# A block pair's first sum and block A22's low part by negated copies and adding DMAs, two more block pairs, and modulation kept off the late tiles

## The chip, the cores and the metric

The kernel runs on one core of a Trainium2 chip. Its engines work side by side, each in the order of its own queue: TensorE (PE) multiplies, VectorE (DVE) and ScalarE (ACT) do elementwise work, GpSimd (POOL) does a little in the attention, SyncE (SP) issues most of the loads, and 16 DMA engines carry them out. The metric is the device time of one execution in microseconds; lower is better.

## What is computed

The reference is a two-layer block stack (width 1024, 256 latent tokens and 256 context tokens). Layer 0 has a short-convolution mixer, layer 1 a grouped-query attention; before and after each mixer stands a gated feed-forward network (FFN). Every step is modulated by vectors that come from `c` and `c_ctx` through `mod_w`. Cut to what matters:

```python
mod  = (silu(c)     @ mod_w[i] + mod_b[i])       # 9 vectors of 1024 per layer, per stream
modc = (silu(c_ctx) @ mod_w[i] + mod_b[i])
h    = rms(t, norm_g) * (1 + scale) + shift      # scale, shift: two of the nine
y    = (silu(h @ w13[:, :2816]) * (h @ w13[:, 2816:])) @ w2
t    = t + 0.5 * gate * y                        # FFN; gate: a third one
t    = t + gate * mixer(h)                       # conv mixer (layer 0), attention (layer 1)
```

Four FFNs run for the latents, three of them for the context as well. The nine vectors of a layer are called channels 0 to 8 here: (shift, scale, gate) for FFN, mixer, FFN. Channels 2 and 8 are the gates with the factor 0.5.

## The kernel before, in words

All of it is float32 in accuracy: a matrix is split in a high part rounded to the format that TensorE takes (`hi`, a ScalarE copy) and a low part (`lo = src - hi`, a VectorE subtraction); a product is three matmuls, `hi*hi`, `hi*lo`, `lo*hi` (`mm3`, lines 127 to 133). `split` (lines 107 to 109) makes the two parts. Tokens are the moving side, 512 of them (256 latents beside 256 context tokens) in all FFNs but the last.

**Weights.** `load_raw` takes one of 8 buffers with the tag `wr` (128 x 1024 float32, 512 KB) and lets SP load it. The parts go to `wh` and `wl`, 4 buffers each, and for block A22 to `w4h`, `w4l`, 2 each.

**FFN.** `ffn` cuts the 22 hidden blocks of 128 in thirds of 8, 7 and 7 (`THIRDS`). For each block the gate and up halves of w13 are multiplied with h, `silu(gate)*up` becomes one entry of `gs`, and `project` multiplies the entries of a third with w2 in 8 output tiles m = 0 to 7 and adds them to x in `finish` (line 547). In the last third the two last tiles are done in halves, first the 256 latents, then the context (`late`), so that the next norm (`tail_norm`) can begin.

**Block pairs.** A hidden block is done in one of two ways. As it is: 8 k-slices x 2 halves x 3 matmuls of 512 columns, 48 in all (`w13_mm`). As a pair (class `Pair`): the gate and up halves and the two halves of k make a 2 x 2 block matrix A, the streams and the halves of k a matrix B, and seven block products instead of eight are done (`head`, `five`, `six`, `seven`, `four`), 84 matmuls of 256 columns. A pair needs sums of blocks: `S1` (line 702), `S2` (703), `S3` and `S4` (711), each then split; `T1` to `T4` of the B side are made once for an FFN. Its two raw tiles are r1 = (A21, A11) and r2 = (A22, A12). `AS_IS` says which blocks of the first third are done as they are: 3 to 7 in the first FFN (blocks 0 to 2 belong to the start), none elsewhere, where blocks 0 and 1 are done as they are by hand. That makes 54 pairs.

**Modulation.** A unit is one dot product of 1024 for 128 outputs of one channel and stream on VectorE (`mod_unit`, line 173, tile `junk`); 218 of them run through the queue `jobs`, 4 (later 2) to a job, and each job loads 1 MB into two `wr` buffers. `tick(n)` adds n to what is owed and issues that many units at that place of the program; `mod_ready` issues what is missing of a channel. `tick(ev)` stands behind every tile of `project` but the late ones, `tick(4)` behind a block done as it is, `tick(5)` behind a tile of the convolution, `tick(0.5)` behind a pair.

The order of the instructions on an engine is fixed when the program is built: a planner takes, by its own times, what is ready, the earlier in the program the sooner. The start (up to 60 us) and the attention heads have an order written by hand. At run time an engine that waits for one instruction holds all behind it.

Of the kernel before, what the change touches and what calls it, by code (L numbers as in the profile page):

```python
# [9 lines left out]
F32 = mybir.dt.float32  # L10
# [13 lines left out]

AS_IS = {(0, 0): range(3, 8), (0, 1): (), (1, 0): ()}

# [21 lines left out]
def hybrid_kernel(ctx: ExitStack, tc: tile.TileContext, a: dict, out: bass.AP):  # L48
# [58 lines left out]
    def split(hi, lo, src):  # L107
        nc.scalar.activation(out=hi, in_=src, func=AF.Copy)  # L108
        return nc.vector.tensor_tensor(out=lo, in0=src, in1=hi.bitcast(F32), op=ALU.subtract)  # L109

    def half():

        return tuple(
            wp.tile([P, 1024], F32R, name=nm(t), tag=t, bufs=4) for t in ("wh", "wl")
        )
# [51 lines left out]
    def mod_unit(l, ch, pair, raw, j, v):  # L167

        mt = mod_tile(l, ch)
        kt = pair * 2 + j  # L170
        col = ch * KT + kt
        junk = mp.tile([P, D], BF16, name=nm("junk"), tag="junk", bufs=1)
        nc.vector.tensor_tensor_reduce(  # L173
            out=junk,
            in0=raw[j],
            in1=scbc[:, v, :],
            scale=1.0,
            scalar=modb[:, l, col : col + 1],
            op0=ALU.mult,
            op1=ALU.add,  # L180
            accum_out=mt[:, kt, v : v + 1],
        )
        done[l, ch] += 1
# [49 lines left out]
    def gate_of(l, j):  # L233
        m = mod_ready(l, 3 * j + 2)
        if j == 1:
            return m
        t = const.tile([P, KT, 2], F32, name=f"G{l}{j}", tag=f"G{l}{j}")
        nv = 1 if (l, j) == (1, 2) else 2
        nc.vector.tensor_scalar(
            out=t[:, :, :nv], in0=m[:, :, :nv], scalar1=0.5, scalar2=None, op0=ALU.mult  # L240
        )
        return t

# [303 lines left out]
    def finish(m, ps, c0, c1, gate, tail, wide=False):  # L547
        g = gate()
        for s in range(2):
            for o in [s * S - c0] if not wide else range(0, T2 if s == 0 else 0, S):  # L550
                if not c0 <= s * S < c1:
                    continue
                nc.vector.scalar_tensor_tensor(  # L553
                    out=x[:, m, s * S : s * S + S],
                    in0=ps[:, o : o + S],
                    scalar=g[:, m, s : s + 1],
                    in1=x[:, m, s * S : s * S + S],
                    op0=ALU.mult,
                    op1=ALU.add,
                )  # L560
        if tail:
            tail(m, c0, c1)
# [6 lines left out]
    def project(ws, src, nk, gate, tail, tot, late, ev, between=()):  # L569
# [37 lines left out]
        for m in range(nf, KT - late):  # L607
# [6 lines left out]
            finish(m, ps, 0, tot, gate, tail, wide)  # L614
            tick(ev)
        if late:
# [58 lines left out]
    class Pair:  # L675
# [6 lines left out]
        def __init__(self, src, h):  # L682
            self.h, self.w = h, {}
            self.raw = [load_raw(src[:, c : c + 1024]) for c in (0, 1024)]
            ts = half()
# [10 lines left out]
        def sums(self, n):  # L696
# [4 lines left out]
            if n == 0:  # L701
                tt(out=s1, in0=s1, in1=r2[:, :T2], op=ALU.subtract)
                tt(out=s2, in0=s2, in1=s1, op=ALU.subtract)
# [4 lines left out]
            ]  # L708
            split(*self.w["A22"], r2[:, :T2])
            v = lambda t: t.rearrange("p (a c) -> p a c", a=2)  # L710
# [42 lines left out]

    def ffn(l, b, h, tot, gate, tail, gs=(), ev=1.5, z=None):
        gs = list(gs)
        i0 = 0
        for t, n in enumerate(THIRDS):
            between = ()
            if tot == T2:
# [22 lines left out]
                for i in range(len(gs), n):  # L782
                    if t == 0 and not heads and i in AS_IS[l, b]:
# [14 lines left out]
                        w13_post(pp, gs[-1], 0, T2)  # L798
                        tick(4)
                        continue  # L800
# [46 lines left out]
            def ws2(m):  # L847
# [12 lines left out]
                else lambda k, c0, c1: (cur[k][0][:, c0:c1], cur[k][1][:, c0:c1]), n,  # L860
                gate, tail if end else None, tot, 2 if end and tot == T2 else 0, ev, between,
            )
            gs = []

    def lazy_gate(l, j):
        box = []

        def get():
            if not box:
                box.append(gate_of(l, j))  # L870
            return box[0]

        return get

# [172 lines left out]
    for i in range(3):  # L1047
        gs0.append(new_pair("g"))
        w13_post(pps[i], gs0[i], 0, T2)

    with tc.issue_after(rows["last"]):
        convk = cload("convk", [P, 3, KT])
# [6 lines left out]
    hn = Plain()  # L1059
    ffn(0, 0, h, T2, lazy_gate(0, 0), tail_norm(0, 1, hn), gs0, 2)  # L1060
    h = hn

    zs = []
    for m in range(KT):
# [4 lines left out]
        for c0, c1 in ((0, S), (S, T2)) if m == 0 else ((0, T2),):  # L1069
# [13 lines left out]
        d = tp.tile([P, T2], F32, name=nm("d"), tag="gm", bufs=3)  # L1083
        nc.vector.tensor_scalar(
            out=d, in0=u, scalar1=convk[:, 1, m : m + 1], scalar2=None, op0=ALU.mult
        )
        u2 = u.rearrange("p (s t) -> p s t", s=2)
# [15 lines left out]
    def by_pairs(key, box=None):  # L1103
# [236 lines left out]
    with tc.manual_schedule(engines={e.engine for e in (nc.tensor, nc.vector, nc.scalar, nc.gpsimd)}):  # L1340
# [31 lines left out]
    project(  # L1372
        by_pairs("wo", wos), lambda k, c0, c1: aos[k], KT, lazy_gate(1, 1), tail_early(1, 2, hn, hz), S, 0, 0,
    )
    ffn(
        1, 1, hn, S, lazy_gate(1, 2),
        lambda m, c0, c1: nc.sync.dma_start(out[m], x[:, m, :S]), z=hz,
# [81 lines left out]
```

## Time and profile before

| | |
|---|---|
| median of 3 runs | 1571.84 us (1570.1 to 1575.39) |
| the profiled execution | 1571.47 us |
| its span, first to last instruction | 1569.7 us |
| granted TensorE clock, mean | 0.998 |
| busy: TensorE / VectorE / ScalarE / GpSimd | 1557.7 / 1333.4 / 733.8 / 25.4 us |
| DMA: moved, mean rate | 248.80 MB, 159 GB/s |

Matmuls overlap in the records (a row shows 0.28 us for one that starts 0.12 us after the one before), so TensorE's busy time says only that no long hole is left in it; the start-to-start time of matmuls gives their pace, and the views by stage show where holes and a lower clock are. The queue of a stage can be full on VectorE without costing time; what counts is which wait ends last before a matmul.

### The profile page before, as it was taken

To read this page: it belongs to the slowest core of one execution; us is meant where nothing else is said; L and a number is where in the kernel's file an instruction comes from. 1 tells how busy PE (TensorE), PEld (TensorE's weight loads), DVE (VectorE), ACT (ScalarE), POOL (GpSimd) and SP (SyncE) were. 2 spreads that over 40 slices of the span, in tenths; PEclk is the share of its full clock that TensorE was granted. 3 is DMA by queue.
4 is the path that set the end of the run, shared out by engine and by line. 5 is a ranking of instruction groups with operands and counts; after the bars stand their busy time and mean duration, and the time that the engine had idled before them with its cause. 6 is when DMAs were issued, how large, how long until landed. Compare 5 with 4: busy or idle time off the path is not lost.

```text
span 1569.7 us, 25671 instructions
## 1 busy us (share of the span) xinstructions
PE 1557.7 (99%) x10210; PEld 1422.0 (91%) x10210; DVE 1333.4 (85%) x2129; ACT 733.8 (47%) x1213; POOL 25.4 (2%) x20
## 2 busy tenths in 40 slices
PE   9999999999999999999999999999999999999999
PEld 7888998999888899989899899999899889898888
DVE  5998789899997698978989989969978887887676
ACT  5622452545322365435345465435345445674553
POOL 0000000000000000000000000000000002300000
PEclk9999999999999999999999999999999999999999
DMA  9675246355565323542533614533733853366562
GB/s 373 224 237 180 89 132 187 107 173 159 194 209 166 114 75 108 177 146 87 189 126 117 196 41 135 187 108 118 239 112 114 265 154 106 123 207 221 171 199 75
DMA packets 72120, 248.80 MB, mean 159 GB/s; under 512 B 9024, under 2 KB 10816, under 8 KB 72000
## 3 DMA queue, kind: packets, MB, share of 16 engines
q1 hardware_dynamic: 69408, 245.40, 48.0%
q10 hardware_dynamic: 2592, 1.76, 0.4%
q8 instruction: 80, 1.31, 0.3%
q14 instruction: 40, 0.33, 0.1%
HBM read 244.77 MB, written 1.05 MB: 157 GB/s over the span
## 4 chain that ended last, share of the span: by engine, by line
PE 88%; DVE 6%; DMA 2%; ACT 2%; issue 1%; POOL 0%; POOLq 0%; SPq 0%; ACTq 0%; DVEq 0%
PE py L131 8%; PE py L132 8%; PE py L133 8%; PE p L131 6%; PE p L133 6%; PE p L132 6%; PE q L133 5%; PE q L131 4%; PE q L132 4%; PE py L139 2%; PE pu L139 2%; PE pg L139 2%; PE pg L132 1%; PE pg L133 1%; DMA wr<-in_w 1%; PE pu L132 1%
## 5 line engine op out<-in xcount | busy, mean ns | idle before, releaser
L108 ACT ACTIVATE wh<-wr 128x1024 fp32r<-128x1024 f32 (+2 forms) x442 | 393.7, 916 | 361.9 <-PE py L132 119.6
L109 DVE TENSOR_TENSOR wl<-wr,wh 128x1024 fp32r<-128x1024 f32 (+2 forms) x442 | 454.5, 1048 | 95.1 <-ACT wh L108 76.2
L173 DVE CUSTOM_DVE_ANT_0 junk<-wr,scbc,modb 128x1024 bf16<-128x1024 f32 x218 | 279.4, 1282 | 15.2 <-DMA wr<-in_modT 13.1
L131 PE MATMUL py<-gh,wh 128*128 128x512 f32 (+1 forms) x570 | 214.7, 377 | 0.0
L132 PE MATMUL py<-gl,wh 128*128 128x512 f32 (+1 forms) x570 | 214.0, 375 | 0.0
L133 PE MATMUL py<-gh,wl 128*128 128x512 f32 (+1 forms) x570 | 213.9, 375 | 0.0
L133 PEld LDWEIGHTS py<-gh,wl 128*128 128x128 f32 x570 | 108.3, 190 | 19.0
L131 PEld LDWEIGHTS py<-gh,wh 128*128 128x128 f32 x570 | 108.5, 190 | 18.4
L132 PEld LDWEIGHTS py<-gl,wh 128*128 128x128 f32 x570 | 108.5, 190 | 18.2
L131 PE MATMUL p<-th,wh 128*128 128x256 f32 x432 | 122.3, 283 | 0.0
L132 PE MATMUL p<-tl,wh 128*128 128x256 f32 x432 | 122.3, 283 | 0.0
L133 PE MATMUL p<-th,wl 128*128 128x256 f32 x432 | 122.2, 283 | 0.0
L553 DVE SCALAR_TENSOR_TENSOR x<-py,G,x 128x256 f32<-128x256 f32 x189 | 83.5, 479 | 36.3 <-PE py L133 25.1
L133 PE MATMUL q<-bh,wl 128*128 128x256 f32 x320 | 91.5, 286 | 0.1
L131 PE MATMUL q<-bh,wh 128*128 128x256 f32 x320 | 90.9, 284 | 0.4 <-ACT wh L108 0.4
L132 PE MATMUL q<-bl,wh 128*128 128x256 f32 x320 | 90.5, 283 | 0.0
L132 PEld LDWEIGHTS p<-tl,wh 128*128 128x128 f32 x432 | 82.8, 192 | 0.3
L131 PEld LDWEIGHTS p<-th,wh 128*128 128x128 f32 x432 | 82.8, 192 | 0.3
L133 PEld LDWEIGHTS p<-th,wl 128*128 128x128 f32 x432 | 82.8, 192 | 0.0
L108 ACT ACTIVATE w4h<-wr 128x512 fp32r<-128x512 f32 x54 | 33.8, 625 | 75.1 <-DMA wr<-in_w 56.9
L108 ACT ACTIVATE gh<-gm 128x512 fp32r<-128x512 f32 x66 | 41.6, 630 | 56.0 <-DVE gm L751 53.8
L711 DVE TENSOR_TENSOR wr<-wr,wr 128x1024 f32<-128x1024 f32 x54 | 66.0, 1222 | 0.7
(303 smaller groups left out, 3946.3 us busy)
## 6 DMA issues: line engine op xcount, KB each, us to landing
wr<-in_w SPq DMA_DIRECT2D x176, 512.0 KB, 4.5
wr<-in_modT SPq DMA_DIRECT2D x122, 512.0 KB, 4.5
wr<-in_w2b SPq DMA_DIRECT2D x64, 448.0 KB, 3.9
wr<-in_w2a SPq DMA_DIRECT2D x32, 512.0 KB, 4.7
pm<-in_mod SPq DMA_DIRECT2D x16, 512.0 KB, 10.2
wr<-in_cw_cx SPq DMA_DIRECT2D x16, 512.0 KB, 4.7
wr<-in_cw_b SPq DMA_DIRECT2D x8, 512.0 KB, 4.4
wr<-in_cw_out SPq DMA_DIRECT2D x8, 512.0 KB, 3.9
```

Of the source, the lines that this page charges most:

```text
L108: nc.scalar.activation(out=hi, in_=src, func=AF.Copy)
L109: return nc.vector.tensor_tensor(out=lo, in0=src, in1=hi.bitcast(F32), op=ALU.subtract)
L131: nc.tensor.matmul(ps, wh, mh, start=first, stop=False, **kw)
L132: nc.tensor.matmul(ps, wh, ml, start=False, stop=False, **kw)
L133: nc.tensor.matmul(ps, wl, mh, start=False, stop=last, **kw)
L139: nc.tensor.matmul(ps, w[0], m[2], start=first and n == 0, stop=False)
L173: nc.vector.tensor_tensor_reduce(out=junk, in0=raw[j], in1=scbc[:, v, :], scale=1.0, scalar=modb[:, l, col : col + 1], op0=ALU.mult, op1=A ...
L553: nc.vector.scalar_tensor_tensor(out=x[:, m, s * S : s * S + S], in0=ps[:, o : o + S], scalar=g[:, m, s : s + 1], in1=x[:, m, s * S : s * ...
L711: tt(out=v(r2), in0=v(r2), in1=s2.unsqueeze(1).to_broadcast([P, 2, T2]), op=ALU.subtract,)
```

## The change

It consists of these edits:

- **S1 without VectorE.** `Pair.__init__` loads r2 whole and of r1 only the second half (A11). The first half of r1 is written by ScalarE as `-A22` (a copy of r2's first half with scale -1), and a DMA from GpSimd's queue adds A21 to it from memory (`accum_op=add`). The VectorE subtraction of line 702 goes.
- **A22's low part without VectorE.** `split_far` has ScalarE copy `hi` and then `-hi` into `lo`, and a DMA from GpSimd's queue adds A22 to it, read a second time from memory.
- **Two more pairs.** `AS_IS` of the first FFN is blocks 3 to 5; blocks 6 and 7 become pairs (56 pairs).
- **Ticks.** No tick behind tile 5 of a `project` with late tiles, nor behind tiles 6 and 7 of one without. `ev` is given for the first two thirds and the last one apart: (2.9, 2.4) instead of 2, (2.7, 2) instead of 1.7, (2.5, 1.6) instead of 1.5; 1.8 instead of 1.5 behind the convolution; `tick(3)` instead of `tick(4)` behind a block done as it is.
- **Gates.** A gate is asked for tile by tile (the units of two tiles at a time) instead of whole before the first tile; the factor 0.5 goes into the unit's scale and, once, into the bias, so the tiles `G` and their scaling go.
- **Convolution.** The middle tap `d` (line 1084) is made by ScalarE instead of VectorE.

```diff
-AS_IS = {(0, 0): range(3, 8), (0, 1): (), (1, 0): ()}
+AS_IS = {(0, 0): range(3, 6), (0, 1): (), (1, 0): ()}
...
+    def split_far(hi, lo, raw, src):
+        nc.scalar.activation(out=hi, in_=raw, func=AF.Copy)
+        nc.scalar.activation(out=lo, in_=hi.bitcast(F32), func=AF.Copy, scale=-1.0)
+        nc.gpsimd.dma_start(out=lo, in_=src, accum_op=ALU.add)
...
-            scale=1.0,
+            scale=0.5 if ch in (2, 8) else 1.0,
...
     def gate_of(l, j):
-        m = mod_ready(l, 3 * j + 2)
...
+        ch = 3 * j + 2
+        def get(m):
+            while done.get((l, ch), 0) < (m // 2 + 1) * 2 * streams(l, ch):
+                next_unit()
+            return modv[l, ch]
+        return get
...
             finish(m, ps, 0, tot, gate, tail, wide)
-            tick(ev)
+            if m < (5 if late else 6):
+                tick(ev)
...
         def __init__(self, src, h):
-            self.h, self.w = h, {}
-            self.raw = [load_raw(src[:, c : c + 1024]) for c in (0, 1024)]
+            self.h, self.w, self.src = h, {}, src
+            r2 = load_raw(src[:, 1024:2048])
+            r1 = wp.tile([P, 1024], F32, name=nm("wr"), tag="wr", bufs=8)
+            nc.sync.dma_start(r1[:, T2:], src[:, T2:1024])
+            nc.scalar.activation(out=r1[:, :T2], in_=r2[:, :T2], func=AF.Copy, scale=-1.0)
+            nc.gpsimd.dma_start(out=r1[:, :T2], in_=src[:, :T2], accum_op=ALU.add)
+            self.raw = [r1, r2]
...
             if n == 0:
-                tt(out=s1, in0=s1, in1=r2[:, :T2], op=ALU.subtract)
                 tt(out=s2, in0=s2, in1=s1, op=ALU.subtract)
...
-            split(*self.w["A22"], r2[:, :T2])
+            split_far(*self.w["A22"], r2[:, :T2], self.src[:, 1024 : 1024 + T2])
...
-                        tick(4)
+                        tick(3)
...
+    for ch in (2, 8):
+        b = modb[:, :, ch * KT : ch * KT + KT]
+        nc.vector.tensor_scalar(out=b, in0=b, scalar1=0.5, scalar2=None, op0=ALU.mult)
...
-    ffn(0, 0, h, T2, lazy_gate(0, 0), tail_norm(0, 1, hn), gs0, 2)
+    ffn(0, 0, h, T2, gate_of(0, 0), tail_norm(0, 1, hn), gs0, (2.9, 2.4))
...
-        nc.vector.tensor_scalar(
-            out=d, in0=u, scalar1=convk[:, 1, m : m + 1], scalar2=None, op0=ALU.mult
-        )
+        nc.scalar.activation(out=d, in_=u, func=AF.Copy, scale=convk[:, 1, m : m + 1])
...
-        lazy_gate(0, 1), tail_norm(0, 2, hn), T2, 2, 1.5,
+        gate_of(0, 1), tail_norm(0, 2, hn), T2, 2, 1.8,
...
-    ffn(0, 1, h, T2, lazy_gate(0, 2), tail_norm(1, 0, hn), (), 1.7)
+    ffn(0, 1, h, T2, gate_of(0, 2), tail_norm(1, 0, hn), (), (2.7, 2))
...
-    ffn(1, 0, h, T2, lazy_gate(1, 0), tail_norm(1, 1, hn), (), 1.5)
+    ffn(1, 0, h, T2, gate_of(1, 0), tail_norm(1, 1, hn), (), (2.5, 1.6))
```

More of the change, by code (lines that the diff above doesn't have):

```diff
@@ L233, in gate_of @@
     def gate_of(l, j):
-        m = mod_ready(l, 3 * j + 2)
[L235 to L238, printed above, removed]
-        nc.vector.tensor_scalar(
-            out=t[:, :, :nv], in0=m[:, :, :nv], scalar1=0.5, scalar2=None, op0=ALU.mult
-        )
-        return t
+        ch = 3 * j + 2
[4 more added lines that the diff above has]
+        return get
     accs = {}
@@ L547, in finish @@
     def finish(m, ps, c0, c1, gate, tail, wide=False):
-        g = gate()
+        g = gate(m)
         for s in range(2):
@@ L752, in four, with ffn @@
             split(g[0], g[1], self.gm)
-    def ffn(l, b, h, tot, gate, tail, gs=(), ev=1.5, z=None):
+    def ffn(l, b, h, tot, gate, tail, gs=(), ev=(0, 0), z=None):
         gs = list(gs)
@@ L860, in ffn @@
                 else lambda k, c0, c1: (cur[k][0][:, c0:c1], cur[k][1][:, c0:c1]), n,
-                gate, tail if end else None, tot, 2 if end and tot == T2 else 0, ev, between,
+                gate, tail if end else None, tot, 2 if end and tot == T2 else 0, ev[end], between,
             )
             gs = []
[L865 to L873, printed above, removed]
     h = Plain()
@@ L1083, in hybrid_kernel @@
         d = tp.tile([P, T2], F32, name=nm("d"), tag="gm", bufs=3)
-        nc.vector.tensor_scalar(
-            out=d, in0=u, scalar1=convk[:, 1, m : m + 1], scalar2=None, op0=ALU.mult
-        )
+        nc.scalar.activation(out=d, in_=u, func=AF.Copy, scale=convk[:, 1, m : m + 1])
         u2 = u.rearrange("p (s t) -> p s t", s=2)
@@ L1372, in hybrid_kernel @@
     project(
-        by_pairs("wo", wos), lambda k, c0, c1: aos[k], KT, lazy_gate(1, 1), tail_early(1, 2, hn, hz), S, 0, 0,
+        by_pairs("wo", wos), lambda k, c0, c1: aos[k], KT, gate_of(1, 1), tail_early(1, 2, hn, hz), S, 0, 0,
     )
     ffn(
-        1, 1, hn, S, lazy_gate(1, 2),
+        1, 1, hn, S, gate_of(1, 2),
         lambda m, c0, c1: nc.sync.dma_start(out[m], x[:, m, :S]), z=hz,
```

## The prediction

> **What bounds the kernel now.** I read the page first, then the windows by stage, then the chain and the timeline where a window was not full.
>
> ```profile
> span 1569.7 us, 25671 instructions
> PE 1557.7 (99%) x10210; PEld 1422.0 (91%) x10210; DVE 1333.4 (85%) x2129; ACT 733.8 (47%) x1213; POOL 25.4 (2%) x20
> ```
>
> TensorE shows 12.0 us of holes in 1569.7 us. The kernel is bound by its matmuls, so it can win by fewer or shorter matmuls, by those 12 us, and by TensorE's clock; what VectorE saves counts only where a matmul waits for VectorE. The windows (columns: length, then busy time of PE, PEld, DVE, ACT, POOL, granted clock, DMA share, GB/s) say where the holes are.
>
> ```profile
> 0.00:60.00 60.00, 57.78 (x389) 45.66 (x390) 42.01 (x101) 36.87 (x67) 0.19 (x4) 1.00 0.88 335
> ...
> 1240.00:1300.00 60.00, 57.65 (x364) 52.91 (x363) 50.25 (x95) 29.02 (x48) 0.00 (x0) 0.94 0.57 178
> 1300.00:1360.00 60.00, 58.22 (x434) 53.15 (x433) 47.54 (x112) 38.45 (x90) 25.20 (x16) 1.00 0.28 87
> 1360.00:1570.00 210.00, 206.32 (x1318) 187.50 (x1317) 156.30 (x258) 111.05 (x190) 0.00 (x0) 1.00 0.55 175
> ...
> 1256.80:1258.60 1.80, 0.28 (x4) 0.07 (x2) 1.69 (x4) 0.00 (x0) 0.00 (x0) 1.00 0.18 75
> 1259.60:1266.50 6.90, 6.90 (x35) 6.90 (x34) 4.41 (x13) 2.93 (x6) 0.00 (x0) 0.51 0.50 144
> 700.00:757.00 57.00, 56.98 (x475) 56.78 (x474) 44.84 (x63) 31.11 (x54) 0.00 (x0) 1.00 0.29 88
> 757.00:800.00 43.00, 42.96 (x212) 36.30 (x211) 41.61 (x67) 13.01 (x18) 0.00 (x0) 1.00 0.64 206
> ```
>
> The start, the attention and the last FFN, which the change leaves alone, hold 2.2 + 1.8 + 3.7 = 7.7 us of the 12.0. The window 1240 to 1300, the end of the third FFN, holds 2.35 us, and it is the only one with a lower clock. All the rest, some 1180 us with all the pairs, has 2.0 us (holes under 0.16 us are hidden in the records, where a matmul of 0.12 us shows as 0.28). A pair stage (700 to 757) leaves TensorE 0.02 us idle with VectorE at 79%; a `project` stage (757 to 800) 0.04 us with VectorE at 97%. So a full VectorE by itself costs nothing today.
>
> The chain of waits and VectorE's and TensorE's timeline, around 1256 us:
>
> ```profile
> 1251.56 5.22 DMA wr<-in_modT
> 1256.91 1.28 DVE L173 CUSTOM_DVE_ANT_0 junk<-wr,scbc,modb 128x1024 bf16<-128x1024 f32 x1 [2.39 <-DMA wr<-in_modT]
> 1258.60 0.38 PE L268 MATMUL ss<-ones,acc 128*128 128x1 f32 x2 [1.52 <-DVE acc L259]
> ```
>
> A modulation unit, ticked behind tile 5, stands in VectorE's queue ahead of the last sum of squares. Its load is issued only at 1251.56 and takes 5.22 us, VectorE waits 2.39 us for it, and TensorE, in the late tiles, waits 1.52 us behind that. One microsecond later the granted clock falls to half, and stays there for 6.9 us.
>
> **The change, part by part.** The sum is made against the profiled execution, 1571.47 us (span 1569.7 and 1.8 around it), 0.4 us under the median of 1571.84.
>
> *Two more pairs.* From TensorE's timeline, six 512-column matmuls from start to start and twelve of 256:
>
> ```profile
> 63.11 0.39 PE L131 MATMUL pg<-hh,wh 128*128 128x512 f32 x1
> ...
> 64.47 0.39 PE L131 MATMUL pg<-hh,wh 128*128 128x512 f32 x1
> ...
> 711.77 0.28 PE L131 MATMUL q<-th,wh 128*128 128x256 f32 x1
> ...
> 713.21 0.28 PE L131 MATMUL p<-th,wh 128*128 128x256 f32 x1
> ```
>
> 1.36/6 = 0.227 us and 1.44/12 = 0.120 us. A block as it is takes 48 x 0.227 = 10.90 us, a pair 84 x 0.120 = 10.08: 0.82 us each, **-1.6 us** for two. Their sums on VectorE have room, since ticks of 4 + 4 + 4 + 4 + 4 become 3 + 3 + 3 + 0.5 + 0.5 there: ten units fewer, 13 us.
>
> *The unit ahead of the last tiles.* There is no tick behind tile 5 any more, so the last unit is ticked a tile earlier, and the sums of squares stand behind no unit. Gone are the 1.52 us and half the speed for 6.9 us, 0.49 x 6.9 = 3.4 us: **-5.0 us**. Bounds: nothing (the load is late all the same, one place earlier) and -5.0. I take the whole, because the tile between gives VectorE 40 matmuls, 40 x 0.120 = 4.8 us, twice its wait of 2.39 us. What is late next is the chain of the norm itself (sum, root, scaling), which stays.
>
> *VectorE and ScalarE in the pairs.* The rows, with the mean of one:
>
> ```profile
> L702 DVE TENSOR_TENSOR wr<-wr,wr 128x512 f32<-128x512 f32 x54 | 37.2, 688 | 12.8 <-DMA wr<-in_w 12.6
> L109 DVE TENSOR_TENSOR w4l<-wr,w4h 128x512 fp32r<-128x512 f32 x54 | 37.1, 687 | 1.2 <-ACT w4h L108 1.0
> L108 ACT ACTIVATE w4h<-wr 128x512 fp32r<-128x512 f32 x54 | 33.8, 625 | 75.1 <-DMA wr<-in_w 56.9 <-PE p L132 18.2
> L1084 DVE TENSOR_SCALAR d<-u,convk x8: 479/483/487, 402.5 to 510.4; 128x512 f32<-128x512 f32 x8
> ```
>
> VectorE loses 37.2 + 37.1 us, and 8 x 0.48 = 3.9 us in the convolution. ScalarE gains 56 x 2 x 0.625 = 70 us, and about 5 us for eight taps, so 734 becomes some 810. In the pair stage above (five pairs) that is VectorE 44.8 - 6.9 = 37.9 and ScalarE 31.1 + 6.3 = 37.4 of 57: neither is the bound. Off the path, since TensorE lacked 0.02 us there: **0**; bounds -2.0 (all the holes left in these stages) and +2.0 (as much again, as the planner's order changes). [...]
>
> *The adding DMAs.* The trace has none, so they are bounded: landing times of plain loads, and the time from where the parts are made today to the matmul that takes them.
>
> ```profile
> wr<-in_w SPq DMA_DIRECT2D x176, 512.0 KB, 4.5
> cosT<-in_cosT ACTq DMA_DIRECT2D x1, 128.0 KB, 3.1
> 786.24 0.68 DVE L702 TENSOR_TENSOR wr<-wr,wr 128x512 f32<-128x512 f32 x1
> 790.04 0.68 DVE L703 TENSOR_TENSOR wr<-wr 128x512 f32<-128x512 f32 x1
> 803.75 0.28 PE L131 MATMUL q<-th,wh 128*128 128x256 f32 x1
> 1201.53 0.68 DVE L109 TENSOR_TENSOR w4l<-wr,w4h 128x512 fp32r<-128x512 f32 x1
> 1216.51 0.28 PE L131 MATMUL p<-th,w4h 128*128 128x256 f32 x1
> ```
>
> One moves 256 KB and reads its target too: between 3.1 us (128 KB, plain) and 9.0 us (512 KB twice); I take 4.5, the row nearest to 256 KB read from both sides. These two pairs are the tightest: the first sum ends 3.1 us before its next step, but that is 13.0 us before the matmul; A22's low part ends 14.3 us before its matmul. With 0.6 us for the negated copy, 5.1 us (at most 9.6) fit under 14.3, and for the sum a wait of 2 us on VectorE is left, under 13.0. **0**, at 9.0 too. If that cover went, every pair would pay the excess. [...] The bytes are 256 KB more for a pair, 15 MB beside 249, on engines busy for 0.29 of the pair stage. SP issues as many loads as before.
>
> *Ticks and gates.* As many units as before, but 15 to 18 in the first six tiles of a third instead of 12 to 16 in eight (the ticks added up). From the stage 757 to 800:
>
> ```profile
> L173 DVE CUSTOM_DVE_ANT_0 junk<-wr,scbc,modb 128x1024 bf16<-128x1024 f32 x13 | 16.7, 1282 | 0.1
> L109 DVE TENSOR_TENSOR wl<-wr,wh 128x896 fp32r<-128x896 f32 x8 | 8.5, 1087 | 1.3 <-ACT wh L108 1.3
> L553 DVE SCALAR_TENSOR_TENSOR x<-py,G,x 128x256 f32<-128x256 f32 x14 | 5.9, 477 | 0.0
> ```
>
> A tile of the first third is 24 matmuls of 0.227 us, 5.45 us. VectorE's part of it: 2 x 0.48 + 1.09 + 2.9 x 1.28 = 5.8 us, so up to 0.3 us late a tile, 1.9 us after six, and given back in the two tiles without units. A product waits for `finish` only when six PSUM banks are full: **0**, bounded by 1.9 us in each of nine thirds, +17. The gate's units are done before they are asked for (added up likewise), and the scaling that goes was 3 tiny instructions. Two halvings of the bias come in, off the path.
>
> Sum: 1571.5 - 1.6 - 5.0 = **1565 us** (0.43% faster).
>
> **The rivals.** *The wait only moves.* SP gets a `wr` buffer for the last unit's load when an earlier unit is done; if that stays so, VectorE waits just as long a tile earlier, the root waits with it, and the clock falls again. For it: the load was issued the moment a unit ended (1251.56). Against it: the tile between. Then only the pairs count, 1571.5 - 1.6 = 1570 us.
>
> *Slower by the adding DMAs.* GpSimd's queue is in order: A22's DMA can stand behind that of a later pair's sum, whose negated copy waits for a raw load. Such waits exist:
>
> ```profile
> ACT w4h L108 <- DMA wr<-in_w: 56.9, 16, 9.6
> ```
>
> 16 waits, 3.6 us in the mean, 9.6 at the longest. With a mean wait, the chain 3.6 + 0.6 + landing passes the 14.3 us from a landing of 10 us on; the longest does so from 4.1 us. If five of the sixteen came out 5 us late at TensorE, that is 1571.5 - 6.6 + 25 = 1590 us. Against it: the raw loads mostly lie far ahead, and two landings of 4.5 us fit in a pair's 10.08 us one behind the other.
>
> *Slower by a full VectorE.* The `project` stages are at 97%, and the units are pressed together there. If 12 of the 17 us above reach TensorE, and the wait at the norm stays, the time is 1571.5 - 1.6 + 12 = 1582 us; it decides from where VectorE falls behind by more than the PSUM banks hold. GpSimd could add to it. In the attention it works beside VectorE:
>
> ```profile
> 1349.74 3.11 POOL L1297 TENSOR_SCALAR pn<-e,r 128x512 f32<-128x512 f32 x2 [1.20 <-PE pt L1310]
> 1350.16 0.81 DVE L109 TENSOR_TENSOR wl<-wr,wh 128x512 fp32r<-128x512 f32 x1
> 1352.21 0.68 DVE L109 TENSOR_TENSOR wl<-wr,wh 128x512 fp32r<-128x512 f32 x1
> ```
>
> A VectorE subtraction begun inside GpSimd's work took 0.81 us instead of 0.68: 0.13 more, at 112 DMAs 15 us, less than the 74 saved. [...]
>
> **How the numbers follow.** Chances: the forecast 0.55 (1561 to 1569: the two bounds of 2.0 us and two for the rest), the wait only moves 0.20, a full VectorE 0.13, the adding DMAs 0.12. A measurement of this kernel tells about 0.3% from no change, here 4.7 us: under 1567.1 is faster, over 1576.6 slower. Most of the first case is faster (0.50 of 0.55); its rest and the second case are the same, 0.25; the last two are slower, 0.25. The range from 1561 to 1582 holds the first two cases and half of the third, 0.81; the likeliest case alone has 1561 to 1569.
>
> **What would show it.** Right: the window 1240 to 1270 with the clock at 1.00 and no VectorE wait for `in_modT` ahead of `acc`; 56 pairs, and for blocks 6 and 7 84 matmuls of 256 columns each in place of 48 of 512; VectorE near 1265 us, ScalarE near 810; adding DMAs that land within 9 us and TensorE as full as now from 600 to 1240. Wrong: a clock of 0.5 anywhere between 60 and 1360 us, TensorE waiting for `w4l` or `wr`, or `x<-py` that waits in VectorE's queue with PSUM full.

## The result: 0.7% slower, and the profile after

The changed kernel takes 1584.26 us (median of four runs, 1582.14 to 1584.5) beside 1572.26 us of the kernel before: a ratio of 1.0072 with a 95% interval of 1.0052 to 1.0091. A second measurement, taken as a mark for the experiments, gives 1.0073 (1.0060 to 1.0086). The forecast was 1565 us. The profiled execution took 1582.14 us. Below, "so many us over the kernel before" is always the ratio less 1, times 1570 us; the changed kernel is 11.4 us over.

The page of the changed kernel, first lines, DMA queues and DMA issues:

```profile
span 1580.4 us, 26335 instructions
PE 1558.5 (99%) x10282; PEld 1426.4 (90%) x10282; DVE 1279.5 (81%) x2023; ACT 801.8 (51%) x1345; POOL 123.1 (8%) x132
...
q1 hardware_dynamic: 69408, 230.72, 45.6%
q0 software_dynamic: 16128, 29.37, 11.3%
...
wr<-in_w POOLq DMA_DIRECT2D x56, 256.0 KB, 4.9
w4l<-in_w POOLq DMA_DIRECT2D x56, 256.0 KB, 5.9
```

The work moved about as forecast: VectorE lost 54 us (68 forecast), ScalarE gained 68 (76 forecast), and the adding DMAs land in 5 to 6 us in the median. TensorE has 21.9 us of holes instead of 12.0. The windows say where (columns as before: length, busy PE, PEld, DVE, ACT, POOL, clock, DMA share, GB/s):

```profile
100.00:110.00 10.00, 8.19 (x56) 7.99 (x55) 9.03 (x13) 4.10 (x7) 0.00 (x0) 0.83 0.31 88
278.00:288.00 10.00, 7.11 (x46) 6.68 (x45) 7.95 (x11) 4.75 (x9) 1.73 (x2) 0.83 0.77 181
1160.00:1170.00 10.00, 7.47 (x60) 7.07 (x60) 7.37 (x9) 5.55 (x10) 1.72 (x2) 1.00 0.55 125
...
700.00:757.00 57.00, 56.23 (x469) 56.02 (x468) 41.20 (x54) 33.86 (x61) 6.09 (x7) 1.00 0.51 124
1240.00:1300.00 60.00, 57.01 (x349) 51.34 (x348) 49.28 (x98) 28.64 (x48) 0.00 (x0) 0.97 0.54 172
```

The first three windows in the kernel before:

```profile
100.00:110.00 10.00, 10.00 (x45) 8.28 (x45) 9.74 (x16) 3.17 (x4) 0.00 (x0) 1.00 0.72 223
278.00:288.00 10.00, 10.00 (x84) 9.91 (x84) 9.17 (x15) 4.67 (x8) 0.00 (x0) 1.00 0.49 159
1160.00:1170.00 10.00, 10.00 (x86) 10.00 (x85) 6.08 (x10) 5.34 (x10) 0.00 (x0) 1.00 0.18 63
```

TensorE lacks 1.8, 2.9 and 2.5 us in the first three windows, all full in the kernel before, and the clock of 0.83 costs 1.7 us more in two of them. The stage from 700 lost 0.8 us where it had lost 0.02, and the end of the third FFN has its wait still. The view of waits names what was late:

```profile
ACT wr L695 <- DMA wr<-in_w: 80.9, 28, 7.8
...
DVE junk L179 <- DMA wr<-in_modT: 29.0, 28, 5.0
...
PE p L137 <- ACT sg L740: 4.6, 2, 2.9
PE q L137 <- ACT gm L746: 4.0, 4, 1.8
PE ss L274 <- DVE acc L265: 2.5, 2, 2.2
```

No matmul waits for `w4l`, the low part that an adding DMA completes. TensorE waits for `sg` and `gm`, the small copies by which ScalarE reads a partial product out of PSUM, the memory in which TensorE adds up, before TensorE adds the next product onto it there (lines 740 and 746). And ScalarE waits 80.9 us for raw loads in front of the negated copy (line 695). The timeline around 281 us puts the two together:

```profile
261.80 0.33 SPq L104 DMA_DIRECT2D wr<-in_w  x1
265.12 0.33 SPq L693 DMA_DIRECT2D wr<-in_w  x1
273.37 0.33 SPq L104 DMA_DIRECT2D wr<-in_w  x1
...
269.32 0.63 ACT L695 ACTIVATE wr<-wr 128x512 f32<-128x512 f32 x1 [7.79 <-DMA wr<-in_w]
269.86 1.04 ACT L108 ACTIVATE wh<-wr 128x1024 fp32r<-128x1024 f32 x1
...
277.55 0.63 ACT L695 ACTIVATE wr<-wr 128x512 f32<-128x512 f32 x1 [3.10 <-DMA wr<-in_w]
...
280.73 0.63 ACT L695 ACTIVATE wr<-wr 128x512 f32<-128x512 f32 x1 [1.51 <-DVE wl L109]
281.27 0.35 ACT L740 COPY sg<-p 128x256 f32<-128x256 f32 x1
...
281.68 0.39 PE L137 MATMUL p<-th,wh 128*128 128x256 f32 x1 [2.89 <-ACT sg L740]
```

ScalarE's queue was planned with the negated copies of three or four later pairs ahead of the first pair's `sg`. The first of those shown waits 7.79 us for a load issued at 261.80. Behind it stands the split of an earlier pair's S1 and S2 (269.86); S3 and S4, and so the release of that pair's raw buffers, wait for that; SyncE's next load goes only at 273.37, and the next negated copies wait for their loads in turn. At the end of the queue `sg`, 0.35 us of work, comes 2.89 us late for TensorE.

The hole at 105 us is of another kind (timelines of SyncE, VectorE, ScalarE and TensorE):

```profile
94.30 0.33 SPq L104 DMA_DIRECT2D wr<-in_modT  x1
...
93.05 1.23 DVE L109 TENSOR_TENSOR wl<-wr,wh 128x1024 fp32r<-128x1024 f32 x1
99.29 1.28 DVE L179 CUSTOM_DVE_ANT_0 junk<-wr,scbc,modb 128x1024 bf16<-128x1024 f32 x1 [5.02 <-DMA wr<-in_modT]
...
102.91 0.69 DVE L715 TENSOR_TENSOR wr<-wr 128x512 f32<-128x512 f32 x1
...
103.77 1.06 ACT L108 ACTIVATE wh<-wr 128x1024 fp32r<-128x1024 f32 x1 [1.92 <-DVE wr L715]
104.73 0.35 ACT L746 COPY gm<-q 128x256 f32<-128x256 f32 x1
...
105.14 0.39 PE L137 MATMUL q<-hh,wh 128*128 128x256 f32 x1 [1.81 <-ACT gm L746]
```

The subtraction at 93.05 frees the raw buffer that the unit's load needs. The load goes when it ends (94.30), VectorE waits 5.02 us for it, and S2 of the second new pair (line 715) stands behind; ScalarE's split of that sum waits for it, and `gm` of the first new pair stands behind the split. The chain of waits has the same thing at the norm near 1270 us, where the wait was forecast to go:

```profile
1263.15 5.96 DMA wr<-in_modT
...
1269.13 1.28 DVE junk L179
...
1270.82 0.38 PE ss L274 x2
```

### The profile page after: what moved, and what is told of

It reads as the page before. It is cut to its first block, busy times and chain, and to the rows that moved or that the text cites. A ratio compares the mean times of both kernels' runs of the same rounds, so it can differ in the third digit from the quotient of the medians.

```text
span 1580.4 us, 26335 instructions
## 1 busy us (share of the span) xinstructions
PE 1558.5 (99%) x10282; PEld 1426.4 (90%) x10282; DVE 1279.5 (81%) x2023; ACT 801.8 (51%) x1345; POOL 123.1 (8%) x132
## 3 DMA queue, kind: packets, MB, share of 16 engines
q1 hardware_dynamic: 69408, 230.72, 45.6%
q0 software_dynamic: 16128, 29.37, 11.3%
HBM read 259.45 MB, written 1.05 MB: 165 GB/s over the span
## 5 line engine op out<-in xcount | busy, mean ns | idle before, releaser
L179 DVE CUSTOM_DVE_ANT_0 junk<-wr,scbc,modb 128x1024 bf16<-128x1024 f32 x222 | 284.5, 1281 | 31.8 <-DMA wr<-in_modT 29.0
L137 PE MATMUL p<-th,wh 128*128 128x256 f32 x448 | 127.3, 284 | 4.6 <-ACT sg L740 4.6
L139 PE MATMUL p<-th,wl 128*128 128x256 f32 x448 | 127.1, 284 | 0.0
L138 PE MATMUL p<-tl,wh 128*128 128x256 f32 x448 | 127.0, 283 | 0.0
L559 DVE SCALAR_TENSOR_TENSOR x<-py,mod,x 128x256 f32<-128x256 f32 x213 | 94.2, 479 | 34.5 <-PE py L139 23.3
L696 POOL DMA_DIRECT2D wr<-in_w x56 | 48.8, 872 | 829.9 <-ACT wr L695 672.5
L695 ACT ACTIVATE wr<-wr 128x512 f32<-128x512 f32 x56 | 35.2, 629 | 117.5 <-DMA wr<-in_w 80.9
L137 PEld LDWEIGHTS p<-th,wh 128*128 128x128 f32 x448 | 86.1, 192 | 5.4 <-ACT sg L740 5.0
L138 PEld LDWEIGHTS p<-tl,wh 128*128 128x128 f32 x448 | 86.1, 192 | 0.4
L139 PEld LDWEIGHTS p<-th,wl 128*128 128x128 f32 x448 | 86.1, 192 | 0.0
```

Of the source, the lines that this page charges most:

```text
L137: nc.tensor.matmul(ps, wh, mh, start=first, stop=False, **kw)
L138: nc.tensor.matmul(ps, wh, ml, start=False, stop=False, **kw)
L139: nc.tensor.matmul(ps, wl, mh, start=False, stop=last, **kw)
L179: nc.vector.tensor_tensor_reduce(out=junk, in0=raw[j], in1=scbc[:, v, :], scale=0.5 if ch in (2, 8) else 1.0, scalar=modb[:, l, col : col ...
L559: nc.vector.scalar_tensor_tensor(out=x[:, m, s * S : s * S + S], in0=ps[:, o : o + S], scalar=g[:, m, s : s + 1], in1=x[:, m, s * S : s * ...
L695: nc.scalar.activation(out=r1[:, :T2], in_=r2[:, :T2], func=AF.Copy, scale=-1.0)
```

## The experiments

Theory "held queue": the negated copies hold ScalarE's queue. Rivals: "late landing" (the adding DMAs themselves reach TensorE) and "full VectorE". All versions are timed in five rounds beside the kernel before.

### Both parts undone, one by one

```diff
 # s1_vector: S1 by VectorE, r1 loaded whole
-            nc.scalar.activation(out=r1[:, :T2], in_=r2[:, :T2], func=AF.Copy, scale=-1.0)
-            nc.gpsimd.dma_start(out=r1[:, :T2], in_=src[:, :T2], accum_op=ALU.add)
...
+                tt(out=s1, in0=s1, in1=r2[:, :T2], op=ALU.subtract)
 # a22_vector: A22's low part by VectorE; both_vector: both edits
-            split_far(*self.w["A22"], r2[:, :T2], self.src[:, 1024 : 1024 + T2])
+            split(*self.w["A22"], r2[:, :T2])
```

> The changed kernel with S1 made by VectorE again: r1 is loaded whole, the negated copies and the adding DMAs for S1 are gone, those for A22's low part stay. Theory 'held queue' (in the trace of the changed kernel the negated copy stands in ScalarE's queue, waits there for its raw load, 28 times and 80.9 us in all, and holds the PSUM copies sg and gm that TensorE waits for): the holes ahead of sg and gm near 105, 281, 706 and 1165 us go (about 2.0 + 3.1 + 0.9 + 2.8 = 8.8 us), and with them two spells of half clock of 3.4 us (1.7 us each): 1584.3 - 12 = 1572, give or take 2. Theory 'late landing' (the adding DMAs reach TensorE): half of them stay, about 1578. Theory 'full VectorE': 56 x 0.69 = 38 us more on VectorE, 1584 or more.

> The changed kernel with A22's low part made by VectorE again; S1's negated copies and adding DMAs stay. Held queue: the copies that wait for loads all stay, 1583 give or take 2, with holes ahead of sg and gm as large as now. Late landing: half of the adding DMAs go, about 1578. Full VectorE: 38 us more on VectorE, 1584 or more.

> The changed kernel with S1 and A22's low part both made by VectorE again; two more pairs, ticks, gates and the convolution as changed. Held queue and late landing: 1572 give or take 2, no more than the version with S1 alone on VectorE by the first, some 6 us less than it by the second. Full VectorE: 77 us more on VectorE where the units are pressed together, 1590 or more.

Measured: 1.0029 (1.0016 to 1.0042), 1.0033 (1.0020 to 1.0046) and 1.0029 (1.0017 to 1.0041): 4.6, 5.2 and 4.6 us over the kernel before. "Full VectorE" falls: work given back to VectorE makes it faster. "Held queue" misses the second: without A22's part the S1 copies still wait for loads (33 times, 77 us), yet 6 us are gone. It misses the other two by less: it had them level with the kernel before, give or take 2 us. "Late landing" misses the third, since undoing either part is worth as much as undoing both. By the times, either part alone adds next to nothing to both_vector. By the profiles, a22_vector still has 2.0 us of holes ahead of `sg` and `gm`, s1_vector 0.6 us and both_vector none.

### The order of the copies

```diff
 # copies_later; lag4 has 4 in place of 2; heads_done holds the first sg copy of every pair
-            nc.scalar.activation(out=r1[:, :T2], in_=r2[:, :T2], func=AF.Copy, scale=-1.0)
+            with tc.issue_after(heads_done[-2]) if len(heads_done) >= 2 else nullcontext():
+                nc.scalar.activation(out=r1[:, :T2], in_=r2[:, :T2], func=AF.Copy, scale=-1.0)
```

> The changed kernel with one ordering added: a pair's negated copy stands in ScalarE's queue behind the sg copy of the pair two before it. The same work on every engine and the same DMAs. Held queue: 1572 give or take 2, and the holes ahead of sg and gm gone. Late landing: no better, 1584 or more, since the adding DMAs start later. Full VectorE: 1584.

> The changed kernel with the smallest change of order: a pair's negated copy stands in ScalarE's queue behind the sg copy of the pair four before it. In the changed kernel seven of the 56 first sg copies stand behind the negated copy of the fourth pair after them, whose raw load can only take the buffers of the pair that is being multiplied; these seven places are moved by one, the others stay up to three pairs ahead. The large holes of both profiles of the changed kernel (at 278 to 282, 702 to 706, 811, 1164 to 1168 us) stand at such places. If that is the cause ('the fifth pair's load'): these holes go, 8 us and a spell of half clock, 2 to 4 us over the kernel before. If the copies hold ScalarE's queue wherever they wait, or A22's adding DMAs slow the loads as such: within 3 us of the changed kernel, 9 us or more over the kernel before.

Measured: copies_later 1.0012 (1.0001 to 1.0022), 1.9 us over the kernel before; the same work and the same DMAs, 9.6 us less than the changed kernel (0.0073 less 0.0012). lag4 1.0063 (1.0038 to 1.0088): the theory of the fifth pair's load fell. The timeline of lag4 shows why:

```profile
279.04 0.38 PE L137 MATMUL p<-th,wh 128*128 128x256 f32 x1 [1.02 <-ACT sg L745]
...
282.93 0.58 PE L137 MATMUL q<-hh,wh 128*128 128x256 f32 x1 [2.20 <-ACT gm L751]
...
280.51 0.63 ACT L698 ACTIVATE wr<-wr 128x512 f32<-128x512 f32 x1 [1.53 <-DVE wl L109]
281.56 1.06 ACT L108 ACTIVATE wh<-wr 128x1024 fp32r<-128x1024 f32 x1 [0.42 <-ACT wr L698]
282.53 0.35 ACT L751 COPY gm<-q 128x256 f32<-128x256 f32 x1
```

`sg` now stands one place ahead and the hole there shrinks from 2.89 to 1.02 us. The moved copy stands in front of `gm` instead, which comes 2.20 us late.

### Copy or DMA

```diff
 # a22_copy_vector
         nc.scalar.activation(out=lo, in_=hi.bitcast(F32), func=AF.Copy, scale=-1.0)
-        nc.gpsimd.dma_start(out=lo, in_=src, accum_op=ALU.add)
+        nc.vector.tensor_tensor(out=lo, in0=raw, in1=lo.bitcast(F32), op=ALU.add)
 # a22_copy_aside: the same, and behind S1's DMA (`dma`)
...
+            with tc.issue_after(dma.ins):
+                nc.gpsimd.dma_start(out=aside, in_=src[:, 1024 : 1024 + T2], accum_op=ALU.add)
```

> The changed kernel with ScalarE still making the high part and the negated copy of A22, but VectorE adding the raw block to it in place of the adding DMA: ScalarE's work as in the changed kernel, 56 DMAs fewer, 38 us more on VectorE. The version with A22 wholly by the old split was 5.2 us over the kernel before, though its S1 copies still waited for loads (33 times, 77 us), against what 'held queue' expected. If ScalarE's second copy is what counted, this one stays 9 to 12 us over the kernel before; if A22's adding DMA is (VectorE's work being no gain), 3 to 7 us over.

> The version with VectorE adding to A22's negated copy (1.7 us over the kernel before), with an adding DMA of the same 256 KB put back behind S1's in GpSimd's queue, into a tile that nobody reads. Nothing in the computation waits for it; the order of ScalarE's copies is that of the version without it. If A22's adding DMA costs by its traffic (in the changed kernel the raw load of pair 11 landed 7.4 to 8.3 us after its issue, beside two adding DMAs, against 5.0 us without A22's, and ScalarE's negated copy waits for that load): most of the 10 us comes back, 7 to 12 us over the kernel before, with that load at 7 us or more. If it costs because A22's low part comes late, or by its place in the order: 1 to 3 us over the kernel before.

> The changed kernel once more, beside more runs of the kernel before, as the mark for the versions made from it: 11.3 us over the kernel before (the first measurement, of four runs, has a factor of 1.0072). If its large holes (near 105, 281, 706, 1165 and 1271 us) are of its order of instructions, they stand at the same places again; if they are chance of one execution, others stand there.

Measured: a22_copy_vector 1.0011 (1.0001 to 1.0021), 1.7 us over, less than either case of its expectation; a22_copy_aside 1.0092 (1.0076 to 1.0109), 14.4 us over, more than expected. ScalarE does the same work in both as in the changed kernel. A DMA whose result nobody reads brings the loss back; so it is its traffic, not A22's low part coming late. The changed kernel's holes came again at 105, 278, 702, 1164 and 1269 us in its second profile, and one more at 811. All four versions load a pair's r2 near 260 us, for the second third of the first FFN. The view of DMA issues, in a window around that load (size, time to landing), for the changed kernel (second profile):

```profile
wr<-in_w SPq DMA_DIRECT2D x1, 512.0 KB, 8.3
w4l<-in_w POOLq DMA_DIRECT2D x1, 256.0 KB, 8.8
```

for a22_copy_vector:

```profile
wr<-in_w SPq DMA_DIRECT2D x1, 512.0 KB, 5.0
```

for a22_copy_aside:

```profile
wr<-in_w SPq DMA_DIRECT2D x1, 512.0 KB, 7.2
aside<-in_w POOLq DMA_DIRECT2D x1, 256.0 KB, 7.5
```

and for copies_later:

```profile
wr<-in_w SPq DMA_DIRECT2D x1, 512.0 KB, 8.2
```

| | over the kernel before | negated copies wait for raw loads |
|---|---|---|
| changed kernel, second profile | 11.4 us | 32 times, 87.0 us, 7.2 at the longest |
| a22_copy_aside | 14.4 us | 32 times, 81.8 us, 7.1 |
| a22_copy_vector | 1.7 us | 30 times, 56.2 us, 4.4 |
| a22_vector | 5.2 us | 33 times, 77.1 us, 6.1 |
| copies_later | 1.9 us | 6 times, 9.7 us, 2.4 |

Beside A22's adding DMA this one load lands in 7.2 to 8.3 us, without it in 5.0. Over all loads of this kind (`wr<-in_w`) the medians on the pages differ less: with the adding DMA, or the one that nobody reads, 4.6 to 4.7 us for 512 KB and 4.0 to 4.6 for the half load of r1, in a22_copy_vector 4.4 and 3.4. In copies_later the load is as late as in the changed kernel, but ScalarE hardly waits for such loads, and the loss is gone. Traffic makes the loads late, and the place of the negated copies passes it on: a22_copy_vector and copies_later take away one each, and are 9.7 and 9.6 us faster than the changed kernel. The sum of the waits is not the whole measure: a22_vector, also without A22's DMA, has 77.1 us of them and is 3.5 us slower than a22_copy_vector, and what sets these two apart is not shown. GpSimd's queue is not in it: in the changed kernel each of the 56 DMAs of S1 (line 696) starts within 1.04 us of the start of its negated copy. In a22_copy_aside a DMA that nobody reads also waits 19 times for the one before it, 52.9 us in all; whether the 3 us above the changed kernel come from that, or from noise, stays open, since the intervals overlap.

### The pairs, the ticks, the gates

```diff
 # pairs_alone: the kernel before with
-AS_IS = {(0, 0): range(3, 8), (0, 1): (), (1, 0): ()}
+AS_IS = {(0, 0): range(3, 6), (0, 1): (), (1, 0): ()}
 # ticks_alone: both_vector with range(3, 8); old_ticks: that, with the ticks of the kernel before
-            if m < (5 if late else 6):
-                tick(ev)
+            tick(ev)
...
-                        tick(3)
+                        tick(4)
...
-    ffn(0, 0, h, T2, gate_of(0, 0), tail_norm(0, 1, hn), gs0, (2.9, 2.4))
+    ffn(0, 0, h, T2, gate_of(0, 0), tail_norm(0, 1, hn), gs0, (2, 2))
...
```

> The kernel before with blocks 6 and 7 of the first FFN as pairs, and nothing else. By the paces of the prediction: 1.6 us under the kernel before. Rival 'the first pairs come too early' (in the version with both parts on VectorE a hole of 1.6 us lies ahead of the second pair's A22 matmul at 113 us, with a pair's parts behind modulation units in VectorE's queue): the gain is eaten, between 1 us under the kernel before and 2 us over it, with a hole of 1 us or more between 100 and 116 us.

> The version with both parts on VectorE, with blocks 6 and 7 as they are: what is left of the change are ticks, gates and the convolution tap. The version with the two pairs was 4.2 us over the kernel before. If the pairs bring their 1.6 us, this one is about 6 us over the kernel before; if their gain is eaten, about 4 us; if ticks and gates cost nothing, as the prediction has it, 0 give or take 1. The places to look at: the norms near 556 and 909 us (holes of about 1 us there in the version with the pairs, 0.3 us before) and the wait near 1260 us.

> The version with ticks, gates and the convolution tap alone (4 to 5 us over the kernel before), with the ticks as in the kernel before, so that gates tile by tile and the tap on ScalarE are all that is left of the change. If the ticks' new places are what cost: the kernel before within 1.5 us. If the gates or the tap are: 4 to 5 us over it.

Measured: pairs_alone 1.0005 (0.9992 to 1.0018), with a hole of 0.9 us at 103 us, ahead of the new pairs: no gain is seen. ticks_alone 1.0027 (1.0013 to 1.0041), 4.2 us over; old_ticks 0.9999 (0.9990 to 1.0008). So gates and the tap cost nothing and the ticks' places do, with S1 on VectorE. The clearest place is the window of the second FFN's last norm, ticks_alone first and old_ticks second:

```profile
900.00:912.00 12.00, 10.51 (x75) 9.98 (x75) 7.05 (x16) 5.31 (x9) 0.00 (x0) 0.90 0.29 98
```

```profile
900.00:912.00 12.00, 12.00 (x93) 11.55 (x92) 7.83 (x18) 5.77 (x10) 0.00 (x0) 1.00 0.32 97
```

and in ticks_alone's timeline there:

```profile
902.22 0.69 DVE L709 TENSOR_TENSOR wr<-wr,wr 128x512 f32<-128x512 f32 x1 [2.08 <-DMA wr<-in_w]
...
907.05 0.38 PE L274 MATMUL ss<-ones,acc 128*128 128x1 f32 x2 [0.73 <-DVE acc L265]
```

With no unit behind tile 5 the planner put the next pair's S1 there. It waits 2.08 us for its raw load, ahead of the sum of squares. This window has 1.5 us of holes and 1.2 us of slower clock (0.90 in 12 us) that old_ticks does not have; the two profiled executions are 2.9 us apart. The changed kernel, with S1 off VectorE, lacks 0.06 us from 900 to 915 us, so this loss is not part of its 11.4. For s1_vector and both_vector it may be what is left of their 4.6 us: they have holes of 1.2 and 0.9 us at the norms near 556 us, and of 1.0 and 0.5 us near 910. This is not shown for a22_vector, which has S1 off VectorE.

### Buffers, and the places of the units

```diff
 # after_wr9 (changed kernel), later_wr9 (copies_later), before_wr9, pairs_wr9 (kernel before; pairs_alone)
-        raw = wp.tile([P, 1024], F32, name=nm("wr"), tag="wr", bufs=8)
+        raw = wp.tile([P, 1024], F32, name=nm("wr"), tag="wr", bufs=9)
...
-        cosT = cload("cosT", [P, S])
+        cosT = tp.tile([P, S], F32, name="cosT", tag="ris1", bufs=1)
+        nc.scalar.dma_start(cosT, a["cosT"])
...
 # later_early: copies_later with
-            if m < (5 if late else 6):
-                tick(ev)
+            if m < (4 if late else 6):
+                tick(ev * 1.25 if late else ev)
 # units_behind (changed kernel), later_wr9_behind (later_wr9): first project only
-                tick(ev)
+                with tc.issue_after(added[-1]) if not first else nullcontext():
+                    tick(ev)
```

> The changed kernel with nine wr buffers instead of eight (the room comes from the rope tables, which take two buffers of the first norm). Theory 'loads wait for a buffer': in the changed kernel VectorE waits 5.0 us at 94 us and 3.0 us at 1266 us for a modulation load that is issued only when VectorE's own operation before it frees a buffer (94.3 and 1263.15 us), and the copies on ScalarE wait for raw loads for the same lack; with a ninth buffer the loads are issued earlier, the holes at 105 and 1271 us shrink (up to 2.0 + 1.7 and 2.3 + 1.7 us), those at 281, 706 and 1165 us too (up to 8.5 us): 4 to 12 us under the changed kernel, between 0 and 7 us over the kernel before. Rival 'order of ScalarE's queue alone': the planner places the copies as early as it can whatever the buffers, and the time stays within 3 us of the changed kernel's, 8 to 14 us over the kernel before.

> The version with the copies later, with nine wr buffers as well. If order and buffers are two causes: 1.9 - 6.6 (what the ninth buffer took off the changed kernel) = about 5 us under the kernel before. If both cure the same waits: 0 to 2 us over it, with the hole at 1262 us gone and that at 105 us still there.

> The kernel before with nine wr buffers and nothing else. If the wait at the norm near 1258 us (a hole of 1.7 us, in some executions with half the clock behind it for 6.8 us) is for want of a buffer, it goes: 2 to 5 us under the kernel before. If the load is late for another reason: the same time within 1 us.

> The kernel before with nine wr buffers (1.8 us under the kernel before in its medians, not told apart from it) and with blocks 6 and 7 as pairs. If the ninth buffer frees the place at which the two pairs lose their gain (a hole of 0.9 us at 103 us with eight): 1.6 us more, 3 to 4 us under the kernel before, and the fastest of all. If the hole stays: 1 to 2 us under.

Measured: after_wr9 1.0017 (1.0002 to 1.0032), later_wr9 0.9999 (0.9990 to 1.0007), before_wr9 0.9995 (0.9986 to 1.0003), pairs_wr9 0.9997 (0.9987 to 1.0006). The room for the ninth buffer comes from two small tables, `cosT` and `sinT`, that move into tiles of the first norm (a22_copy_aside has this move too); in before_wr9 both together change nothing that can be told. In the changed kernel they take off about 9 us. TensorE's wait at the norm near 1260 to 1270 us is gone in all four profiles. With the copies later as well the change is level with the kernel before, no better. No version beats the kernel before by more than the measurement can tell.

> The version with the copies later (1.9 us over the kernel before) and with no tick behind tile 4 of a project with late tiles either, its units put into the four tiles ahead (ev times 1.25). If the wait at the norm near 1262 us (a hole of 2.0 us and 6.8 us at half clock, 5.4 us) comes from the last unit's place, it goes: 3 to 4 us under the kernel before. If the load is late wherever the unit stands (the rival 'the wait only moves' of the prediction): within 1.5 us of the version with the copies later.

> The changed kernel with the units that are ticked in the first project kept behind the x additions of their tile in VectorE's queue. In the changed kernel two of them stand before block 5's product there (a unit that waits 5.0 us for its load at 94 us), and the hole at 105 us follows. If that is its cause: the hole goes, 1.6 to 2.0 us and in some executions 1.7 us of half clock, 2 to 4 us under the changed kernel, 8 to 10 us over the kernel before. If the two pairs come too early for another reason, the hole stays, and the time with it.

> The version with the copies later and nine buffers (0.6 us under the kernel before), with the units of the first project behind their tiles as well. Its holes at 103 and 106 us (1.5 and 1.4 us) go if their cause is the units': 2 to 4 us under the kernel before. If it is another, the same as the version without.

Measured: later_early 1.0018 (1.0006 to 1.0031), the same as copies_later; units_behind 1.0093 (1.0074 to 1.0111) and later_wr9_behind 1.0011 (1.0001 to 1.0020), 3 and 2 us above the versions without the edit, by intervals that overlap. An earlier tick does not help the norm: the unit still waits, as VectorE's timeline of later_early shows.

```profile
1261.67 1.28 DVE L179 CUSTOM_DVE_ANT_0 junk<-wr,scbc,modb 128x1024 bf16<-128x1024 f32 x1 [2.27 <-DMA wr<-in_modT]
```

Keeping the units behind their tile removes the hole at 105 us, as expected, and makes a larger one later, where a pair's split is late behind the units (TensorE, units_behind):

```profile
163.31 0.58 PE L139 MATMUL p<-hh,wl 128*128 128x256 f32 x1 [3.16 <-DVE wl L109]
```

## Why the prediction was wrong

- **VectorE and ScalarE in the pairs, 0 within 2.0: the step that failed.** The busy times came near (ScalarE 802 for 810, VectorE 1280 for 1265). But the step asked whether ScalarE had room, and a copy that needs only a raw load costs by where the planner puts it. It named no wait and nothing queued behind it. With the next step it cost 9.6 us, by copies_later. Its 625 ns are those of a one-input copy, the 687 ns that VectorE loses those of a two-input subtraction; the tap `d`, the same work on either engine, took 483 ns on VectorE (kernel before) and 724 on ScalarE (changed kernel).
- **The adding DMAs, 0: right in what was bounded, wrong in what was passed over.** They land in 4.9 and 5.9 us in the median, 8.5 at the longest (8.8 in the second profile), under 9.0, and no matmul waits for `w4l`. The 15 MB were right, but bytes were the wrong measure: by the page 29.37 MB took 11.3% of the DMA engines' time and 230.72 MB took 45.6%, which is 1.9 times the time for a byte, and in the pair stage (700 to 757) the engines are busy for 0.51 of the time instead of 0.29. And the loads that these bytes delay (5.0 to 8.3 us) were not followed to their readers.
- **The unit ahead of the last tiles, -5.0: did not come.** The rival "the wait only moves" was right here, by its own mechanism: the load goes when a unit frees a buffer (1263.15), and the hole is 2.2 us instead of 1.5. later_early and the ninth buffer show that the buffer decides, not the tick. The clock of that window is 0.97 instead of 0.94, 1.8 us in 60, but spells of half clock change from one execution to the next (see below).
- **Two more pairs, -1.6: not seen.** pairs_alone is at 1.0005; a gain of 1.6 us (0.9990) is just outside its interval. The sum found room on VectorE for the new pairs' sums, but a hole of 0.9 us stands there. It is gone in pairs_wr9; even so that version is no faster than before_wr9. TensorE has 14.5 us of holes in pairs_alone beside 12.0 in the kernel before, and 13.8 in pairs_wr9 beside 12.1 in before_wr9 (one profile each): about as much as the gain, spread over several places. Why they come stays open.
- **Ticks and gates, 0, at most 17.** The gates cost nothing (old_ticks). The ticks cost 4.2 us when S1 is on VectorE, but not by tiles that run late: by what the planner puts in a unit's place, as far as the window at 900 us shows.
- **The rivals.** "Slower by the adding DMAs" had the sign and the wait, a negated copy for a raw load; that its time came near (1590 us, by five waits that were assumed) is luck. It had the wrong queue: GpSimd's waits for nothing that matters, and ScalarE's holds the copies that TensorE waits for. "Slower by a full VectorE" named a time close to the result (1582 us), which is luck, and is refuted: VectorE got work back in s1_vector, a22_vector, both_vector and a22_copy_vector, and all four are faster than the changed kernel. GpSimd did not add to it: issuing the 112 DMAs kept it busy for 98.6 us, and VectorE's 128x1024 subtractions took 1222 ns before and 1222 to 1223 after.
- **The whole.** Forecast and result are 18 us apart: 9.6 by the first two steps, 5.0 and 1.6 that did not come, and 1.9 that copies_later still has over the kernel before. With a ninth buffer as well these 1.9 are not seen. Of the signs of being wrong one came, a clock of 0.5 between 60 and 1360 us; TensorE waited neither for `w4l` nor for a raw load.

## What to carry to other kernels

Before moving work to an engine with time to spare, list what stands behind it in that engine's queue: an instruction that waits for a load should not stand ahead of the copies that TensorE waits for. Follow the extra DMA traffic to the loads it slows (5.0 to 8.3 us for one of them here) and to whoever waits for those. Where a load is issued only when a buffer comes free, moving its reader moved the wait here (2.27 us for VectorE in later_early), and with one buffer more TensorE no longer waited behind it.

## What the runs showed of the hardware

- The adding DMAs from GpSimd's queue took the DMA engines 1.9 times the time for a byte of the plain loads (11.3% of it for 29.37 MB, 45.6% for 230.72 MB). Their packets are smaller (1.8 KB in the mean beside 3.3 KB, by the page), and what share is due to that is not shown. At one place a 512 KB load landed in 8.3 us beside two of them, and in 5.0 us beside one.
- Behind a hole of 1.5 to 2.9 us TensorE's clock was granted at half in some places and not in others. In the first profile of the changed kernel it stood at 0.50 for 3.4 us behind the holes that end at 105.14, 281.68 and 1270.82 us (1.81, 2.89 and 2.17 us), and at 1.00 behind the one that ends at 1165.36 us (1.67 us). In the kernel before it stood at 0.51 for 6.9 us behind the 1.52 us at the norm; from 1255 to 1275 us its mean was 0.83 in ticks_alone and in old_ticks. The window behind the hole at 281.68 us in the changed kernel:

```profile
283.10:286.50 3.40, 3.40 (x17) 3.17 (x16) 2.50 (x3) 1.57 (x4) 0.00 (x0) 0.50 0.77 154
```

and a hole of 1.91 us at the norm in pairs_alone, in its timeline and its windows, with the clock at 1.00 behind it:

```profile
1258.43 0.38 PE L268 MATMUL ss<-ones,acc 128*128 128x1 f32 x2 [1.91 <-DVE acc L259]
```

```profile
1255.00:1268.00 13.00, 10.47 (x81) 9.69 (x79) 10.34 (x25) 6.37 (x13) 0.00 (x0) 1.00 0.37 119
```

The second profile of the changed kernel has no spell at 105 or 278 us, where the first has one each: the clock is 1.00 from 100 to 110 and from 277 to 287 us, with 1.45 and 1.05 us of holes in these windows. And it has one at 1165 us (0.51 from 1164.5 to 1168), where the first has none. So such a spell, 1.7 or 3.4 us lost, is not to be counted on in a forecast, in either direction. What sets it off is not shown.
